# Summing two weight blocks by an adding load from GpSimd, in place of a VectorE addition, in a feed-forward with seven products

## The chip, the cores and the metric

The kernel runs on one core of one Trainium2 chip. The metric is the time of the device for one execution of the whole program, in microseconds, as the median of several runs. A core has five engines that work through their own instruction lists in order: PE (matmuls), DVE (VectorE, elementwise), ACT (ScalarE), POOL (GpSimd) and SP (SyncE, which here only issues loads and stores). Loads and stores are carried by 16 DMA engines; a load is issued from SP, or from GpSimd, and lands some microseconds later.

## What is computed

One layer of a decoder on 512 tokens of width 1024, in float32: two attention branches merged by gates, an output projection with a residual, then the part that matters here, a SwiGLU feed-forward, and a last normalization.

```python
u2 = rms_norm(x, norm_ffn_g[i])
g_ff, up_ff = jnp.split(u2 @ w_ffn_in[i], 2, axis=-1)      # 1024 x 5632
x = x + (jax.nn.silu(g_ff) * up_ff) @ w_ffn_out[i]
return rms_norm(x, norm_final_g)
```

## The kernel before

**Matmuls in three parts.** Each float32 operand is split in two: a rounded part hi (ACT, L143) and the rest lo = value - hi (DVE, L144). A product is then three matmuls: hi by hi, hi by lo, lo by hi (L767 to L769 for the feed-forward's first products, L158 to L160 for all others).

**Seven products in place of eight.** The feed-forward runs over 22 blocks of 128 hidden columns (`hidden(i)`, one call is a step below). In a step the gate's and the up part's 1024 x 128 weights, each halved along the input width, form a 2 x 2 block matrix, and the tokens in two halves the other one. The product of the two is made by a scheme with seven block products in place of eight. It needs, besides the loaded blocks, sums of weight blocks. Four weight pairs (hi, lo) are prepared for a step, in this order:

- A1: the loaded gate weights, as they are.
- S23: two blocks. The first is (up block 1 + up block 2) + gate block 1, the second is up block 1 + gate block 1.
- S1: two blocks, the sum (up block 1 + up block 2), and up block 2.
- S4: one block, the first of S23 plus gate block 2.

**Where the sum comes from.** `dma_chunk` (L104) allocates for the up weights a tile `rawu` of three thirds of 512 columns, of which there are two buffers. SP loads the two up blocks into the second and third of them with one load of 512 KB (L108). In `split_chunk` (L116) DVE adds these two into the first third (L133). Then DVE makes S23 from the first two thirds and the gate weights (L135), and later S4 (L140). S1 is read straight from the first and the last third (L137); its subtraction (L144, shown as wlo<-rawu) is the last reader of the tile, so it frees the buffer for the load of two steps later.

**What sets the order.** `weights(i, ahead=2)` (L146) is called by each product for its own weight pair; it first issues the loads up to four weight pairs ahead of the one to be split, and prepares pairs up to two ahead, at high priority. There are three buffers for hi and three for lo, so a cast waits until PE has left the product of three pairs before. On PE the order in the feed-forward is as written (L896). On the other engines, SP's and GpSimd's queues included, a planner sets the order when the kernel is built: it goes by priority and by the times at which it expects operands to be ready. On the chip each engine keeps that order, and waits for semaphores.

**What else is near.** Between the `in` steps stand `out` steps (`down`, L852), plain products with the second weight matrix, one or two after each step from step 6 on. GpSimd has little to do in the feed-forward: the power for the row factors of the normalization (`row_factors`, L276) in step 1 and at the end, and additions of squares at the end (L868). PE waits for the power's result, in its order, at L289.

Of the kernel before, what the change touches and what calls it, by code (L numbers as in the profile page):

```python
# [14 lines left out]
ALU = mybir.AluOpType  # L15

P = 128
S = 512
# [25 lines left out]
def trunk_kernel(ctx, tc, xT, gains, w_in, w_up, w_o, w_f, w_d, bias, out):  # L44
# [5 lines left out]
    nc = tc.nc  # L50
    V, A, G, T = nc.vector, nc.scalar, nc.gpsimd, nc.tensor
# [52 lines left out]
    def dma_chunk(i):  # L104
        kind, ap, n = chunks[i]
        if kind == "S23":
            r = fpool[0].tile([P, 3, S], F32, tag="rawu", name=f"rawu{i}", bufs=2)
            nc.sync.dma_start(out=r[:, 1:3, :].rearrange("p a n -> p (a n)"), in_=ap)  # L108
        elif ap is not None:
            r = wp.tile([P, 1024], F32, tag="raw", name=f"raw{i}", bufs=RAW)  # L110
            nc.sync.dma_start(out=r[:, :n], in_=ap)
        else:
            return
        raws[i] = r

    def split_chunk(i):  # L116
        kind, _, n = chunks[i]
        if i < len(chunks) - 1 and i != first_s4:
            hi = wp.tile([P, 1024], F32R, tag="whi", name=f"whi{i}")
            lo = wp.tile([P, 1024], F32R, tag="wlo", name=f"wlo{i}")  # L120
        else:
            pair_ = wide(f"w{i}", F32R)
            hi, lo = pair_[:, 0, :], pair_[:, 1, :]
        parts[i] = (hi, lo)
        hi, lo = hi[:, :n], lo[:, :n]
        if kind == "plain":
            r = raws.pop(i)[:, :n]
        elif kind == "A1":
            r = raws[i]
        elif kind == "S23":  # L130

            u = raws[i]
            V.tensor_tensor(out=u[:, 0, :], in0=u[:, 1, :], in1=u[:, 2, :], op=ALU.add)  # L133
            r = raws["S23"] = wide(f"s23{i}")
            V.tensor_tensor(out=r, in0=u[:, 0:2, :], in1=raws[i - 1][:, :S].unsqueeze(1).to_broadcast([P, 2, S]), op=ALU.add)  # L135
        elif kind == "S1":
            r = raws.pop(i - 1)[:, 0:3:2, :]  # L137
        else:
            r = fpool[0].tile([P, S], F32, tag="s4", name=f"s4{i}", bufs=1)
            V.tensor_tensor(out=r, in0=raws["S23"][:, 0, :], in1=raws.pop(i - 3)[:, S:], op=ALU.add)  # L140
        if kind in ("S23", "S1"):
            hi, lo = (t.rearrange("p (a n) -> p a n", a=2) for t in (hi, lo))
        A.copy(hi, r)  # L143
        V.tensor_tensor(out=lo, in0=r, in1=hi.bitcast(F32), op=ALU.subtract)  # L144

    def weights(i, ahead=2):  # L146
        with tc.high_priority() if i > 4 else nullcontext():
            while state["split"] <= min(i + ahead, len(chunks) - 1):
                j = state["split"]
                while state["dma"] <= min(j + (2 if chunks[j][0] == "plain" else 4), len(chunks) - 1):  # L150
                    dma_chunk(state["dma"])
                    state["dma"] += 1
                split_chunk(j)
                state["split"] += 1
        return parts[i]
# [34 lines left out]
    def wide(name, dt=F32):  # L190
        return tp.tile([P, 2, S], dt, tag="t4", name=name, bufs=N4)
# [810 lines left out]
```

## Time and profile before

| | |
|---|---|
| median of three runs | 769.46 us (769.3 to 771.01) |
| the profiled execution's own time | 769.63 us |
| its span, first to last instruction | 767.9 us |
| mean granted TensorE clock | 0.996 |
| PE, DVE, ACT, POOL busy | 751.9, 512.7, 360.3, 28.1 us |
| read from HBM | 71.32 MB |

The profile is of one execution. Its times are counted from the first instruction. A row of the timeline gives the start, the length, the engine, the line of the kernel, the operation and its tiles as out<-in; in brackets stands how long the engine had been idle, and what ended that. A row of a group gives count, busy time and mean length, then the idle time in front of it. A row of waits gives the engine and line that waited, what it waited for, microseconds in total, times, and the longest. A tile's name leaves its number out: `rawu` is any of the 22.

### The profile page before, as it was taken

How to read it: one execution, taken by the hardware profiler on the slowest of the kernel's cores; microseconds unless marked ns; L12 is line 12 of the kernel's file. 1: busy time of each engine (PE TensorE's matmuls, PEld its weight loads, DVE VectorE, ACT ScalarE, POOL GpSimd, SP SyncE). 2: the span in 40 equal slices, each digit the busy share in tenths (PEclk: the TensorE clock that was granted, in tenths of full speed). 3: DMA queues.
4: the chain of work that ended last, by engine and by line, in shares of the span. 5: the costliest groups of instructions: out<-in, count | busy, mean ns of one | idle time of the engine just before them, and what ended most of it. 6: DMA issues, size and time to landing. Idle time of an engine off the chain costs nothing. (4 is left out here: it accounts for less than half of the span.)

```text
span 767.9 us, 10991 instructions
## 1 busy us (share of the span) xinstructions
PE 751.9 (98%) x4471; PEld 644.0 (84%) x4471; DVE 512.7 (67%) x694; ACT 360.3 (47%) x515; POOL 28.1 (4%) x39
## 2 busy tenths in 40 slices
PE   8999999999999999999999999999999999999994
PEld 5876767798877878888789999999999999999983
DVE  5443746344677774368798989877788777776543
ACT  7264727563132343233454766544444554444362
POOL 1000000000100100000000000000000000000032
PEclk9999999999999999999999999999999999999998
DMA  7412121123224223233422232323333333331213
GB/s 246 137 56 82 55 83 55 55 78 114 83 84 164 83 83 102 69 103 111 164 83 83 84 103 83 117 76 121 100 103 96 104 103 113 106 107 46 65 46 111
DMA packets 24947, 74.13 MB, mean 97 GB/s; under 512 B 2736, under 2 KB 5824, under 8 KB 24768
## 3 DMA queue, kind: packets, MB, share of 16 engines
q1 hardware_dynamic: 23536, 69.74, 28.2%
q0 software_dynamic: 816, 3.16, 1.2%
q8 instruction: 35, 0.57, 0.3%
q10 hardware_dynamic: 544, 0.52, 0.2%
q14 instruction: 16, 0.13, 0.1%
HBM read 71.32 MB, written 2.10 MB: 96 GB/s over the span
## 5 line engine op out<-in xcount | busy, mean ns | idle before, releaser
L143 ACT CAST whi<-raw 128x1024 fp32r<-128x1024 f32 (+2 forms) x113 | 108.5, 962 | 157.8 <-issue 49.2
L144 DVE TENSOR_TENSOR wlo<-raw,whi 128x1024 fp32r<-128x1024 f32 (+2 forms) x113 | 125.9, 1115 | 37.7 <-ACT whi L143 37.0
L767 PE MATMUL pf<-fh,whi 128*128 128x256 f32 x348 | 99.5, 286 | 0.4 <-ACT q L774 0.4
L769 PE MATMUL pf<-fh,wlo 128*128 128x256 f32 x348 | 98.6, 283 | 0.0
L768 PE MATMUL pf<-fl,whi 128*128 128x256 f32 x348 | 98.5, 283 | 0.0
L767 PE MATMUL pg<-fh,whi 128*128 128x256 f32 x264 | 75.1, 284 | 0.6 <-ACT q L774 0.6
L768 PE MATMUL pg<-fl,whi 128*128 128x256 f32 x264 | 74.7, 283 | 0.0
L769 PE MATMUL pg<-fh,wlo 128*128 128x256 f32 x264 | 74.7, 283 | 0.0
L767 PEld LDWEIGHTS pf<-fh,whi 128*128 128x128 f32 x348 | 66.7, 192 | 2.0 <-ACT q L774 0.9
L768 PEld LDWEIGHTS pf<-fl,whi 128*128 128x128 f32 x348 | 66.7, 192 | 1.1 <-issue 0.5
L769 PEld LDWEIGHTS pf<-fh,wlo 128*128 128x128 f32 x348 | 66.7, 192 | 0.3 <-DVE wlo L144 0.2
L144 DVE TENSOR_TENSOR wlo<-s,whi 128x1024 fp32r<-128x1024 f32 (+1 forms) x43 | 41.2, 959 | 16.0 <-ACT whi L143 15.8
L767 PEld LDWEIGHTS pg<-fh,whi 128*128 128x128 f32 x264 | 50.6, 192 | 1.1 <-ACT q L774 0.8
L143 ACT CAST whi<-s 128x1024 fp32r<-128x1024 f32 (+1 forms) x43 | 36.2, 841 | 31.5 <-PE pg L768 19.6
L769 PEld LDWEIGHTS pg<-fh,wlo 128*128 128x128 f32 x264 | 50.6, 192 | 0.0
L768 PEld LDWEIGHTS pg<-fl,whi 128*128 128x128 f32 x264 | 50.6, 192 | 0.0
L158 PE MATMUL pd<-hh,whi 128*128 128x512 f32 (+1 forms) x132 | 50.4, 381 | 0.0
L159 PE MATMUL pd<-hl,whi 128*128 128x512 f32 (+1 forms) x132 | 50.3, 381 | 0.0
L160 PE MATMUL pd<-hh,wlo 128*128 128x512 f32 (+1 forms) x132 | 50.1, 379 | 0.0
L143 ACT CAST whi<-rawu 128x1024 fp32r<-128x1024 f32 x22 | 23.1, 1050 | 29.6 <-PE pd L159 25.0
L861 DVE TENSOR_TENSOR res<-pd,res 128x512 f32<-128x512 f32 (+1 forms) x36 | 22.6, 628 | 18.9 <-PE pd L160 18.8
L160 PEld LDWEIGHTS pd<-hh,wlo 128*128 128x128 f32 x132 | 24.8, 188 | 4.8
(472 smaller groups left out, 1738.8 us busy)
## 6 DMA issues: line engine op xcount, KB each, us to landing
raw<-in_w_in_dram SPq DMA_DIRECT2D x44, 512.0 KB, 3.3
rawu<-in_w_ffn_in_dram SPq DMA_DIRECT2D x22, 512.0 KB, 3.2
raw<-in_w_ffn_in_dram SPq DMA_DIRECT2D x22, 512.0 KB, 3.3
raw<-in_w_ffn_out_dram SPq DMA_DIRECT2D x24, 384.0 KB, 3.1
raw<-in_w_out_dram SPq DMA_DIRECT2D x8, 512.0 KB, 3.3
raw<-in_w_up_dram SPq DMA_DIRECT2D x8, 384.0 KB, 3.0
x<-in_xT_dram SPq DMA_DIRECT2D x8, 256.0 KB, 4.9
res<-in_xT_dram POOLq DMA_DIRECT2D x8, 256.0 KB, 4.1
```

The lines of the kernel that those rows point to most:

```text
L143: A.copy(hi, r)
L144: V.tensor_tensor(out=lo, in0=r, in1=hi.bitcast(F32), op=ALU.subtract)
L158: T.matmul(ps, shi, mhi, start=first, stop=False)
L159: T.matmul(ps, shi, mlo, start=False, stop=False)
L160: T.matmul(ps, slo, mhi, start=False, stop=last)
L767: T.matmul(ps, hi[:, cs], xhi, start=first and k == 0, stop=False, skip_group_check=True)
L768: T.matmul(ps, hi[:, cs], xlo, start=False, stop=False, skip_group_check=True)
L769: T.matmul(ps, lo[:, cs], xhi, start=False, stop=last and k == 3, skip_group_check=True)
L861: V.tensor_tensor(out=x, in0=ps, in1=x, op=ALU.add)
```

## The change

The addition at L133 goes. The first third of `rawu` is filled by two loads of 256 KB: SP loads up block 1 into it, and GpSimd loads up block 2 with addition into the same place. The old load of both blocks into the other two thirds stays. All lines behind move by two or three.

```diff
@@ dma_chunk
         if kind == "S23":
             r = fpool[0].tile([P, 3, S], F32, tag="rawu", name=f"rawu{i}", bufs=2)
+
+            nc.sync.dma_start(out=r[:, 0, :], in_=ap[:, :S])
+            nc.gpsimd.dma_start(out=r[:, 0, :], in_=ap[:, S:], accum_op=ALU.add)
             nc.sync.dma_start(out=r[:, 1:3, :].rearrange("p a n -> p (a n)"), in_=ap)
@@ split_chunk
             u = raws[i]
-            V.tensor_tensor(out=u[:, 0, :], in0=u[:, 1, :], in1=u[:, 2, :], op=ALU.add)
             r = raws["S23"] = wide(f"s23{i}")
             V.tensor_tensor(out=r, in0=u[:, 0:2, :], in1=raws[i - 1][:, :S].unsqueeze(1).to_broadcast([P, 2, S]), op=ALU.add)
```

## The prediction

> **What bounds the kernel now.** I read the page's first part, then the engines' busy time by stage, then what the tensor engine waited for, then the queues around the changed line.
>
> ```profile
> span 767.9 us, 10991 instructions
> PE 751.9 (98%) x4471; PEld 644.0 (84%) x4471; DVE 512.7 (67%) x694; ACT 360.3 (47%) x515; POOL 28.1 (4%) x39
> ```
>
> ```profile
> 366.00:414.00 48.00, 46.96 (x233) 39.30 (x232) 41.07 (x61) 26.07 (x38) 0.00 (x0) 1.00 0.31 103
> 414.00:482.00 68.00, 67.60 (x546) 65.92 (x545) 61.70 (x100) 41.70 (x69) 1.06 (x1) 1.00 0.30 98
> 482.00:723.00 241.00, 241.00 (x1656) 225.27 (x1655) 181.55 (x259) 113.20 (x172) 0.00 (x0) 1.00 0.31 96
> ```
>
> The columns after the stretch and its length are PE, PEld, DVE, ACT and POOL busy, the clock, the DMA share and GB/s. The changed line runs only in these three stretches. PE is full in the last, and has 1.44 us without a matmul in the first two together. The clock is 1.00. DVE is busy 41.07 of 48.00, then 61.70 of 68.00 (91%), then 181.55 of 241.00 (75%). So DVE is the second-fullest engine, and in the middle stretch it has little room.
>
> ```profile
> PE pg L767 <- ACT q L774: 0.6, 1, 0.6
> PE po L158 <- DVE res L728: 0.4, 1, 0.4
> PE pf L767 <- ACT q L774: 0.4, 1, 0.4
> ```
>
> These are all of PE's waits from 366 to 723 us. None of them is for a feed-forward weight that DVE prepares. Their sum, 1.4 us, is the same as the time without a matmul just read, and the most that a faster preparation could return there.
>
> **What is removed.** The addition at L133, once in each of the 22 steps:
>
> ```profile
> L133 DVE TENSOR_TENSOR rawu<-rawu 128x512 f32<-128x512 f32 x22 | 15.2, 691 | 16.2 <-DMA rawu<-in_w_ffn_in_dram 16.1
> ```
>
> That is 22 x 0.691 = 15.2 us of DVE work, and 16.1 us in which DVE stood at this line until the load had landed. Both are DVE time beside a full PE: DVE's 31.3 us lie under PE's matmuls, and PE waited for none of it. Worth of the removal on the path: 0.
>
> **What is added.** Per step SP issues a 256 KB load into the first third of the tile, GpSimd a 256 KB load that adds into the same bytes, and the old 512 KB load follows.
>
> ```profile
> rawu<-in_w_ffn_in_dram SPq DMA_DIRECT2D x22, 512.0 KB, 3.2
> res<-in_xT_dram POOLq DMA_DIRECT2D x8, 256.0 KB, 4.1
> raw<-in_w_ffn_out_dram SPq DMA_DIRECT2D x8, 256.0 KB, 2.7
> bt<-in_bias_dram POOLq DMA_DIRECT2D x1, 1024.0 KB, 5.1
> ```
>
> Traffic: 22 x 0.5 MB = 11.5 MB in the 357 us from 366 to 723, 32 GB/s on top of some 98, so the DMA share goes from 0.31 to about 0.41, an estimate in proportion. That is far from full, and costs nothing by itself. SP's extra issue stands ahead of the old load, which therefore starts one issue later (the rows below show 0.33 us); the loads queued behind it on SP move by the same.
>
> Latency: the adding load reads what the first one wrote, so GpSimd waits for the landing. The first takes 2.7 us (a 256 KB load of SP). The price of an adding load stands in no row. Its lower bound is a plain 256 KB load of GpSimd, 4.1 us. Its upper bound is two of these after one another, 8.2, if the destination must be fetched first. I take 4.4: it moves the bytes of a 512 KB load, and GpSimd's rows rise by 1.0 us from 256 to 1024 KB, a third of that for 256 KB more. The sum is then complete 2.7 + 4.4 = 7.1 us after SP's issue (6.8 to 10.9), against 3.2 us of load and 0.69 us of addition before.
>
> The serial order is where a rule of the Trainium skill speaks against the change. "DMA: Bandwidth & Descriptors", section "Rules for kernel authors", says that nothing holds the bytes between an accumulating transfer's read and its write, so that it must wait for the earlier transfer's semaphore. By it the two landings add up, as in my sum; were they ordered by the queues alone, the slower one would count. The same page's section "Anatomy of one DMA — SWDGE (gpsimd) path" prices a GpSimd transfer at 2.0 us and the bytes at 436 GB/s, 2.6 us for 256 KB, which would make the chain 5.3; the row measures 4.1 for the plain kind, so the row is what I use.
>
> **Where that latency meets DVE.** The wait moves from L133 to L135, the next reader of the sum, and DVE works in a fixed order: what stands behind L135 waits with it. Here are the steps 4 to 7, in the order load, L135, the subtraction for the step before, and the first matmul that needs its result:
>
> ```profile
> 431.45 0.33 SPq L108 DMA_DIRECT2D rawu<-in_w_ffn_in_dram  x1
> 437.52 1.22 DVE L135 TENSOR_TENSOR s<-rawu,raw 128x1024 f32<-128x1024 f32 x1
> 439.32 1.21 DVE L144 TENSOR_TENSOR wlo<-s,whi 128x1024 fp32r<-128x1024 f32 x1
> 442.42 0.28 PE L769 MATMUL pf<-fh,wlo 128*128 128x256 f32 x1
> ...
> 442.37 0.33 SPq L108 DMA_DIRECT2D rawu<-in_w_ffn_in_dram  x1
> 449.28 1.22 DVE L135 TENSOR_TENSOR s<-rawu,raw 128x1024 f32<-128x1024 f32 x1
> 450.75 1.22 DVE L144 TENSOR_TENSOR wlo<-s,whi 128x1024 fp32r<-128x1024 f32 x1
> 452.65 0.28 PE L769 MATMUL pf<-fh,wlo 128*128 128x256 f32 x1
> ...
> 453.79 0.33 SPq L108 DMA_DIRECT2D rawu<-in_w_ffn_in_dram  x1
> 459.17 1.22 DVE L135 TENSOR_TENSOR s<-rawu,raw 128x1024 f32<-128x1024 f32 x1
> 460.97 1.21 DVE L144 TENSOR_TENSOR wlo<-s,whi 128x1024 fp32r<-128x1024 f32 x1
> 463.58 0.28 PE L769 MATMUL pf<-fh,wlo 128*128 128x256 f32 x1
> ...
> 464.02 0.33 SPq L108 DMA_DIRECT2D rawu<-in_w_ffn_in_dram  x1
> 469.07 1.22 DVE L135 TENSOR_TENSOR s<-rawu,raw 128x1024 f32<-128x1024 f32 x1
> 471.20 1.21 DVE L144 TENSOR_TENSOR wlo<-s,whi 128x1024 fp32r<-128x1024 f32 x1
> 473.80 0.28 PE L769 MATMUL pf<-fh,wlo 128*128 128x256 f32 x1
> ```
>
> The tolerance of a step is the time from its load to that matmul, less the time from L135's start to the subtraction's end. Step 5: 452.65 - 442.37 = 10.28, less 451.97 - 449.28 = 2.69, leaves 7.6 us. Steps 4, 6 and 7 in the same way: 8.0, 6.8 and 6.4. If the DVE order stayed as it is, 7.1 us would be late by 0.3 and 0.7 us in steps 6 and 7 and by nothing in 4 and 5: a mean of 0.25, over seven early steps (2 to 8, the four shown taken for all) 1.8 us.
>
> But L135's own result isn't urgent there. The sum of step 5, made at 449.28, is for a product a full step later, since the subtraction at 450.75 still serves step 4. The order on DVE isn't written out by hand (only PE's is); it is planned from expected times when the kernel is built. L133's place shows that such plans reckon with a load's flight:
>
> ```profile
> DVE rawu L133 <- DMA rawu<-in_w_ffn_in_dram: 16.1, 17, 3.9
> ```
>
> In 17 of 22 steps it waited for the landing, 0.9 us on average, so it stands about where the data is expected. With two flights in a row I expect L135 to be placed some 3 us later, behind the subtractions for the step before, where its wait blocks nothing urgent. The cover is then the rest of a step, about 3 us more. Value taken: 0. If that cover is missing, it costs the 1.8 us above at my latency, and the prices of the first rival at more.
>
> Later steps have more room. From step 9 on L135 stands further from its load; the shortest such distance that I found is step 14's:
>
> ```profile
> 566.96 0.33 SPq L108 DMA_DIRECT2D rawu<-in_w_ffn_in_dram  x1
> 577.02 1.22 DVE L135 TENSOR_TENSOR s<-rawu,raw 128x1024 f32<-128x1024 f32 x1
> ```
>
> 10.06 us, which holds 7.1 and all but the top of its range.
>
> **GpSimd's queue.** It gets 22 waits for a landing. Behind them could stand the row factors' power at L276:
>
> ```profile
> 417.66 0.33 SPq L108 DMA_DIRECT2D rawu<-in_w_ffn_in_dram  x1
> ...
> 423.77 1.06 POOL L276 TENSOR_TENSOR r<-ms,mh 128x4 f32<-128x4 f32 x1 [146.03 <-DVE ms L268]
> ...
> 426.14 1.02 PE L289 MATMUL rb<-dg,ones 128*128 128x512 f32 x2
> ```
>
> PE waits for it, and PE works in order. The load of step 4 can't be issued before PE has gone past that matmul: its buffer comes free with the third weight pair of step 2, whose own buffer PE empties in the last products of step 1, behind the matmul. So the adding load of step 4 can't stand ahead of the power without a deadlock. That of step 3 can be issued at 417.66 + 2.7 = 420.4, 3.4 us before the power. Cost 0, unless GpSimd needs more than those 3.4 us to issue a transfer.
>
> **The sum.** The profiled execution took 769.63 us, of which 767.9 are the span; the median of three is 769.46. 769.63 - 0 + 0 = 769.6 us. A measurement of this kernel tells about 0.3% (2.3 us) from no change.
>
> **Rivals.** First, slower: L135 keeps a place ahead of an urgent subtraction, and the latency exceeds 7.2 us, the mean tolerance of the four steps. Then DVE stands with urgent work behind it and PE stops. At an adding load of 5.5 us the chain is 8.2, the four steps are late by 0.2, 0.6, 1.4 and 1.8 us, mean 1.0; over seven steps 7 us: 777. At the upper bound of 8.2 the chain is 10.9, 3.7 us a step and 26 us, with step 14 and its like touched as well: 796 or more. For it: DVE is 91% busy in this stretch, so little drains a backlog, and in the profile DVE already waited 16.1 us at L133, so the plan's times are somewhat short of the chip's. Against: the urgency lies elsewhere, and the planner can move L135. Chance 0.30, and 0.08 more for an adding load dearer than its upper bound or a late sum in all 22 steps, at 790 and beyond.
>
> Second, faster: DVE, freed of 15.2 us, delivers everything else earlier, and PE's three waits go. That returns at most their 1.4 us: 768.2, still within the bound of no change. A gain over 2.3 us would need PE itself to issue its matmuls faster, for which I see nothing; I leave 0.05 for a new order of the planned engines that helps in the last 45 us, at 767.
>
> Third, the change only moves the wait: DVE's 16.1 us of standing reappear at L135 in the same size or larger, and DVE's idle time isn't smaller. This is compatible with my forecast; it gives 769.6 as well.
>
> **How the numbers follow.** No change 0.57 (769.6, with a gain of 1.4 us or the 1.8 us of the unmoved order still inside 2.3 us), slower 0.30 + 0.08 = 0.38, faster 0.05. The range from 768.0 to 779.0 holds the first case, and the first rival to about 8.5 us of chain, some 0.22 of its 0.30, together 0.79; left out are the dearest cases and a real gain. The likeliest case's own range is 768.0 to 771.8.
>
> **What would show it.** Right: DVE has 22 fewer additions, its busy time is some 15 us lower, PE's rows in 482 to 723 still read 241.00, no wait of PE on wlo appears, and the adding loads land about 4.4 us after issue. Right in part: DVE waits at L135 for the adding load, with no late matmul. Wrong: PEld or PE waits for wlo or for the cast between 410 and 485, a landing above 6 us, or a matmul at L289 that starts late after the power on GpSimd. A time below 767 would mean that DVE had delayed PE in a way that the waits don't show.

## The result, and the profile after

The changed kernel takes 790.89 us (median of 4 runs, 789.99 to 792.56), the kernel before 769.39 us (4 runs). The ratio is 1.0273, with a 95% interval of 1.0260 to 1.0286: slower by 21.5 us, and outside the range of the prediction. The profiled execution took 791.53 us.

The first part of the page after, and the engines' busy time in stretches that answer to the three of before. Columns are as there: PE, PEld, DVE, ACT, POOL, clock, DMA share, GB/s.

```profile
span 789.8 us, 11096 instructions
PE 761.2 (96%) x4471; PEld 649.3 (82%) x4471; DVE 499.6 (63%) x672; ACT 360.1 (46%) x515; POOL 47.3 (6%) x61
```

```profile
366.00:414.00 48.00, 47.83 (x235) 40.06 (x234) 38.28 (x58) 25.14 (x37) 2.26 (x3) 1.00 0.45 137
414.00:504.00 90.00, 75.37 (x553) 71.03 (x552) 60.05 (x95) 43.54 (x72) 6.80 (x8) 0.94 0.40 112
504.00:745.00 241.00, 241.00 (x1656) 225.25 (x1656) 174.08 (x246) 113.21 (x173) 11.23 (x13) 1.00 0.44 124
```

The last stretch is the same as before to the last figure: 241.00 us, 1656 matmuls, PE full, although DMA's share rose from 0.31 to 0.44. So neither the traffic nor the later steps lost time. The middle one grew from 68 to 90 us for some 550 matmuls. In it PE stands 14.63 us, and the granted clock is 0.94. The loads date the loss: at step 1's load on SP the changed kernel's profile is 1.75 us late (367.62 against 365.87), which comes from its start and not from the change (last section); at step 4's it is 11.79 us late (443.24 against 431.45), at step 8's 21.98 (496.23 against 474.25), and 21.9 at the end. So the loss of the change lies between the products of step 1 and those of step 7, one half ahead of step 4's load and one half behind it.

What PE waited for in the changed kernel, with DVE's wait for the new loads (in total, times, longest):

```profile
DVE s L137 <- DMA rawu<-in_w_ffn_in_dram: 23.5, 7, 5.1
...
PE rb L291 <- ACT dg L286: 8.4, 3, 5.6
POOL r L278 <- issue: 7.9, 1, 7.9
...
PE pf L769 <- ACT q L776: 5.5, 3, 2.5
...
PE pf L771 <- DVE wlo L146: 2.1, 3, 1.1
```

L137 is the old L135, the reader of the sum; L291 and L278 are the old L289 and L276. Two places are new. DVE stands 23.5 us at the reader, in 7 of the steps, and PE then waits on what DVE does behind it: 2.1 us on `wlo`, 5.5 us on a PSUM bank (where PE's products collect) that ACT empties into the kept tile `q`, which it can overwrite only when DVE's `g` has read it. And PE waits 5.6 us at once for the row factors, whose power on GpSimd stood 7.9 us without anything that the profile shows to wait for. The loads themselves, by the page (KB each, median us from issue to landing):

```profile
rawu<-in_w_ffn_in_dram SPq DMA_DIRECT2D x22, 512.0 KB, 4.1
...
rawu<-in_w_ffn_in_dram SPq DMA_DIRECT2D x22, 256.0 KB, 3.2
rawu<-in_w_ffn_in_dram POOLq DMA_DIRECT2D x22, 256.0 KB, 3.9
```

**Step 5 in the changed kernel**, from its first load to the late matmuls:

```profile
456.09 0.33 SPq L109 DMA_DIRECT2D rawu<-in_w_ffn_in_dram  x1
...
459.81 0.42 DVE L829 SCALAR_TENSOR_TENSOR u<-q,yv 128x256 f32<-128x256 f32 x1
459.91 0.86 POOL L110 DMA_DIRECT2D rawu<-in_w_ffn_in_dram  x1 [11.80 <-DVE wlo L146]
...
465.37 1.23 DVE L137 TENSOR_TENSOR s<-rawu,raw 128x1024 f32<-128x1024 f32 x1 [5.14 <-DMA rawu<-in_w_ffn_in_dram]
466.51 0.42 DVE L828 TENSOR_TENSOR g<-pg,q 128x256 f32<-128x256 f32 x1
467.02 0.37 ACT L776 COPY q<-pf 128x256 f32<-128x256 f32 x1 [3.97 <-DVE g L828]
...
467.18 1.22 DVE L146 TENSOR_TENSOR wlo<-s,whi 128x1024 fp32r<-128x1024 f32 x1
...
467.44 0.39 PE L769 MATMUL pf<-fh,whi 128*128 128x256 f32 x1 [2.48 <-ACT q L776]
468.45 0.38 PE L771 MATMUL pf<-fh,wlo 128*128 128x256 f32 x1 [0.50 <-DVE wlo L146]
...
468.98 1.22 DVE L146 TENSOR_TENSOR wlo<-rawu,whi 128x1024 fp32r<-128x1024 f32 x1
```

The sum is there 465.37 - 456.09 = 9.3 us after SP's issue. DVE has the reader directly behind `u`, one place earlier than before, where `g` came first. Everything below it in DVE's order waits with it, ACT's copy waits for `g`, and PE stands 2.48 + 0.50 us. The granted clock is then at 0.50 for some 3.4 us. The last row is the subtraction that frees the other of the two buffers. The load of step 6 goes out behind it, at 470.22.

**The row factors**, at the end of step 1's products:

```profile
425.79 0.84 POOL L110 DMA_DIRECT2D rawu<-in_w_ffn_in_dram  x1 [11.38 <-DVE s L142]
...
430.66 0.16 DVE L270 TENSOR_SCALAR ms<-ss 128x4 f32<-128x4 f32 x1
...
434.58 1.05 POOL L278 TENSOR_TENSOR r<-ms,mh 128x4 f32<-128x4 f32 x1 [7.95 <-issue]
...
436.41 2.08 PE L291 MATMUL rb<-dg,ones 128*128 128x512 f32 x2 [5.56 <-ACT dg L286]
```

The power's input is there at 430.82, and the power begins at 434.58, 7.95 us after GpSimd issued its adding load. In the instruction list that the build makes for GpSimd, an instruction of the kind that loads code stands directly ahead of this power. The profile doesn't list it. Before, it stood directly behind the last load of `res` (the residual), at 278 us, in the 146 us that GpSimd idled; in the changed kernel four adding loads stand between that load of `res` and it. What PE does after this wait:

```profile
436.00:438.00 2.00, 1.59 (x3) 0.84 (x3) 1.61 (x7) 1.88 (x5) 0.00 (x0) 0.50 0.00 0
438.00:440.00 2.00, 2.00 (x10) 1.72 (x9) 1.48 (x2) 0.00 (x0) 0.00 (x0) 0.50 0.00 0
440.00:442.00 2.00, 2.00 (x11) 2.00 (x11) 1.63 (x5) 1.07 (x2) 0.00 (x0) 0.50 0.00 0
...
444.00:446.00 2.00, 2.00 (x19) 2.00 (x18) 1.91 (x4) 1.73 (x5) 0.00 (x0) 1.00 0.79 265
```

PE reads as busy, but at a clock of 0.50 it does 10 or 11 matmuls in 2 us instead of 19.

### The profile page after: what moved, and what is told of

The parts are those of the page before. It is cut to its first block, busy times and chain, and to the rows that moved or that the text cites. A ratio compares the mean times of both kernels' runs of the same rounds, so it can differ in the third digit from the quotient of the medians.

```text
span 789.8 us, 11096 instructions
## 1 busy us (share of the span) xinstructions
PE 761.2 (96%) x4471; PEld 649.3 (82%) x4471; DVE 499.6 (63%) x672; ACT 360.1 (46%) x515; POOL 47.3 (6%) x61
## 4 chain that ended last, share of the span: by engine, by line
PE 87%; DMA 5%; DVE 4%; ACT 1%; issue 1%; SPq 0%; POOL 0%; DVEq 0%; POOLq 0%; ACTq 0%
PE pd L160 5%; PE pd L161 5%; PE pd L162 5%; PE pf L771 4%; PE pf L769 4%; PE pf L770 4%; DMA rawu<-in_w_ffn_in_dram 4%; PE pg L769 3%; PE pg L770 3%; PE pg L771 3%; PE pjgs L160 2%; DVE wlo L146 2%; PE pjgd L160 2%; PE pjgs L162 2%; PE pjgd L162 2%; PE po L160 2%
## 5 line engine op out<-in xcount | busy, mean ns | idle before, releaser
L769 PE MATMUL pf<-fh,whi 128*128 128x256 f32 x348 | 101.1, 291 | 6.4 <-ACT q L776 5.5
L137 DVE TENSOR_TENSOR s<-rawu,raw 128x1024 f32<-128x1024 f32 x22 | 26.9, 1222 | 26.0 <-DMA rawu<-in_w_ffn_in_dram 23.5
L110 POOL DMA_DIRECT2D rawu<-in_w_ffn_in_dram x22 | 19.2, 885 | 396.3 <-DMA rawu<-in_w_ffn_in_dram 308.1
```

Source lines behind the costliest of these rows:

```text
L110: nc.gpsimd.dma_start(out=r[:, 0, :], in_=ap[:, S:], accum_op=ALU.add)
L769: T.matmul(ps, hi[:, cs], xhi, start=first and k == 0, stop=False, skip_group_check=True)
```

## The experiments

My theory was that two stalls make the loss: DVE standing at the reader of the sum, and GpSimd's code load that came to lie behind an adding load. Rivals were the traffic itself, the price of an adding load, and, later, each step's lateness taken by itself. The letters in each expectation are those that it defines. Ratios are against the kernel before, run on the same chip, with their 95% intervals. Gains of one changed kernel over another are differences of bare medians; where the two ran in different batches, whose kernels before took 769.4 to 770.6 us, the difference of their excesses is up to 0.7 us larger.

### The power's code loaded early

The changed kernel, with one more small power on GpSimd, of constants, that nothing reads. It stands behind the last load of `res`, so that the code is there before the adding loads.

```diff
+    early = cp.tile([P, 8], F32)
+    pw = G.tensor_tensor(out=early, in0=mh, in1=mh, op=ALU.pow)
+    tc.add_manual_dep(pw.ins, last.ins.name, NOSYNC, reason="issue order")
```

> The change, and a power of eight constants on GpSimd behind the last load of the residual, near 278 us. It makes the code load that stands ahead of the row factors' power happen there, where GpSimd idles. Theory A (two causes: DVE stands at the sum's reader in steps 2 to 8, and GpSimd's code load has moved behind the adding load of step 3, so that PE waits for the row factors and then runs at half clock for a while): the power starts within 0.3 us of its input, PE's wait of 5.6 us at the row factors' matmul shrinks below 2, and 791 falls by 4 to 7 us, to 784 to 787. Rival B (only DVE's standing counts, the power's lateness comes from DVE): no change, 790 to 791. Rival C (the traffic of the extra loads slows the weights down): no change, 790 to 791.

788.2 us, ratio 1.0244 (1.0223 to 1.0264). The timeline of this kernel:

```profile
286.88 1.68 POOL L661 TENSOR_TENSOR early<-mh 128x8 f32<-128x8 f32 x1 [8.27 <-issue]
...
429.35 1.23 DVE L137 TENSOR_TENSOR s<-rawu,raw 128x1024 f32<-128x1024 f32 x1 [4.76 <-DMA rawu<-in_w_ffn_in_dram]
430.49 0.16 DVE L270 TENSOR_SCALAR ms<-ss 128x4 f32<-128x4 f32 x1
...
430.73 1.95 POOL L278 TENSOR_TENSOR r<-ms,mh 128x4 f32<-128x4 f32 x1 [4.90 <-DVE ms L270]
```

The 8.27 us moved to the early power, and the real one now starts 0.08 us after its input. So the pause was the code load, and not work of the adding load. But the input `ms` stands behind the reader on DVE, which waited 4.76 us. So PE still waits 3.3 us there, after which the clock is at half for 6.8 us, and the kernel gains only 2.7 us, where I expected 784 to 787.

### The reader placed later

The changed kernel, with one ordering edge and no semaphore: the reader of the sum stands on DVE behind the subtraction that frees the other buffer (S1 of the step before).

```diff
+            s23 = V.tensor_tensor(...)          # the reader
+            if "after" in state:
+                tc.add_manual_dep(s23.ins, state["after"].ins.name, NOSYNC, reason="issue order")
...
+        sub = V.tensor_tensor(out=lo, in0=r, in1=hi.bitcast(F32), op=ALU.subtract)
+        if kind == "S1":
+            state["after"] = sub
```

> The change, with the sum's reader on DVE held behind the subtraction of the third weight pair of the step before, by an edge for the planner alone. Theory A: DVE's waits for the adding load go to under 2 us, the late steps' PE waits go, but GpSimd's code load still stands behind the adding load of step 3: 776 to 780. Rival B: 769 to 771, since DVE no longer stands. Rival C: 788 to 791.

777.91 us, ratio 1.0111 (1.0096 to 1.0126): 13.0 us of the 21.5 come back. DVE has no wait for `rawu` left. What stays is GpSimd's pause, and PE's wait and half clock behind it:

```profile
431.38 1.05 POOL L282 TENSOR_TENSOR r<-ms,mh 128x4 f32<-128x4 f32 x1 [7.99 <-issue]
...
433.21 2.07 PE L295 MATMUL rb<-dg,ones 128*128 128x512 f32 x2 [4.86 <-ACT dg L290]
```

### Both edits

> The change with both edits, the early power and the late reader. Theory A: 769 to 771, the same as before, with all 22 adding loads in place. Rival B: also 769 to 771. Rival C: 788 to 791, because every byte of the traffic is still there.

771.03 us (10 runs), ratio 1.0014 (1.0004 to 1.0024). The power now starts on its input, behind the same adding load:

```profile
420.59 0.86 POOL L110 DMA_DIRECT2D rawu<-in_w_ffn_in_dram  x1 [8.86 <-DVE u L837]
423.58 1.04 POOL L282 TENSOR_TENSOR r<-ms,mh 128x4 f32<-128x4 f32 x1 [2.14 <-DVE ms L274]
```

All 44 new loads are still there, with all their traffic, and 20 of the 21.5 us are gone. So neither the traffic nor the price of an adding load makes the loss; together they are worth some 1 us (0.3 to 1.8 by the interval). DVE's busy time in this kernel is 500.5 us against 512.7 before, and that brings nothing. The two edits alone give 2.7 and 13.0 us, and together 19.9: the stalls overlap at the row factors, where the reader of step 3's sum holds up the power's input and the code load the power, and each hides part of the other.

### The adding loads only from step 8 on

Steps 0 to 7 keep the old addition.

> The adding loads in steps 8 to 21 only; steps 0 to 7 keep the addition on DVE. Theory A: 769 to 771, since neither the early steps' tight order nor the power's place on GpSimd is touched, with DVE some 9 us less busy; nothing gained, because PE is full there. Rival C: two thirds of the loss stay, 780 to 784.

769.50 us (10 runs), ratio 0.9990 (0.9979 to 1.0002). With the change in fourteen of the 22 steps nothing is lost, and nothing gained.

### One pair of new loads that nobody reads

The kernel before, with the two new loads once, in step 3, into spare bytes. DVE's addition stays. The computation is as before, the two loads are extra work.

```diff
+            if k == 3:
+                x = fpool[0].tile([P, S], F32, tag="form", name=f"spare{i}", bufs=2)
+                new = nc.sync.dma_start(out=x, in_=ap[:, :S])
+                tc.add_manual_dep(new.ins, old.ins.name, NOSYNC, reason="issue order")
+                nc.gpsimd.dma_start(out=x, in_=ap[:, S:], accum_op=ALU.add)
```

> The kernel before, its additions on DVE in place, with one added pair: in step 3 alone SP loads a block into spare bytes that nothing reads, and GpSimd adds another into it. Theory A: the code load for the power stands behind this adding load, the power starts some 8 us after the adding load was issued, about 431, PE waits 4 to 5 us at the row factors' matmul and then runs at half clock for about 6 us: 776 to 779. Rival B (only DVE's standing counts): 769 to 771, since nobody reads the sum.

780.52 us, ratio 1.0127 (1.0112 to 1.0142): a single adding load costs 9.9 us.

```profile
424.28 0.92 POOL L114 DMA_DIRECT2D spare<-in_w_ffn_in_dram  x1 [145.21 <-PE pg L775]
433.87 1.05 POOL L282 TENSOR_TENSOR r<-ms,mh 128x4 f32<-128x4 f32 x1 [8.66 <-issue]
...
435.70 2.07 PE L295 MATMUL rb<-dg,ones 128*128 128x512 f32 x2 [8.17 <-ACT dg L290]
```

It does so only by its place: it stands ahead of the code load, which can now begin at 425.20, and the power starts 8.66 us later. PE waits 8.17 us of them, since here DVE isn't late and nothing else hides the pause. My 776 to 779 were short by 1.5 us at the top: I had taken PE's wait to be 4 to 5 us, near the 5.56 of the changed kernel.

### One flight in place of two

SP's first load left out, and GpSimd's load plain: the first third then holds up block 2 alone and not the sum, so up block 1 is missing where S23, S1 and S4 use the sum of both. DVE's reader stands ahead of the subtractions for the step before, as in the change, and GpSimd's loads have the same places in its queue.

```diff
-            nc.sync.dma_start(out=r[:, 0, :], in_=ap[:, :S])
-            nc.gpsimd.dma_start(out=r[:, 0, :], in_=ap[:, S:], accum_op=ALU.add)
+            nc.gpsimd.dma_start(out=r[:, 0, :], in_=ap[:, S:])
```

> The change without SP's first load, and GpSimd's load plain: one flight in place of two in series, by the same queue, with DVE's addition gone as in the change. The first third then holds the second block alone and not the sum. Theory A (two flights in series are what DVE stands for): DVE's waits at the reader fall from 23.5 us to under 6, the power is late by about 3 us only, since GpSimd needn't wait for a landing; 771 to 776. Rival D (a load on GpSimd's queue is slow or late as such): 784 to 791.

773.01 us, ratio 1.0037 (1.0023 to 1.0050). With one flight DVE waits 2.2 us at the reader in the whole feed-forward. The code load is still late (a pause of 8.12 us), but the load ahead of it is issued at 419.37, without a first flight to wait for, so the power comes at 428.03 and PE waits 2.11 us. So it is the two flights in series that make the change expensive, and not the reader's move to a GpSimd load. The addition went with the first flight here, but it prices little by itself: the median landing is 3.7 us for these plain loads and 3.9 for the adding ones.

### The later reader, with PE kept busy

The kernel with the later reader, and 22 matmuls of zeros on PE ahead of the row factors' matmul, whose result nobody reads.

```diff
+        for _ in range(22):
+            T.matmul(pw, warm, warm.unsqueeze(1).to_broadcast([P, 4, P]), start=True, stop=True)
```

> The late reader of the second experiment, and 22 matmuls of zeros on PE just ahead of the row factors' matmul, some 5 us that fill PE's wait there. They change no result that is read. Theory A with its half clock: PE never stands for long, its clock stays at 1.00, and the about 3 us lost at half clock come back: 777.9 falls to 774 to 776. If the half clock costs nothing, or has another cause: 777 to 779.

775.52 us, ratio 1.0065 (1.0049 to 1.0082), 2.4 us less than without them. The same stretches, first of the kernel with the later reader alone, then of this one:

```profile
432.00:434.00 2.00, 0.79 (x1) 0.50 (x2) 1.50 (x7) 1.54 (x6) 0.43 (x1) 0.50 0.00 0
434.00:436.00 2.00, 2.00 (x7) 1.26 (x6) 1.22 (x4) 0.94 (x2) 0.00 (x0) 0.50 0.00 0
```

```profile
432.00:434.00 2.00, 2.00 (x8) 0.86 (x7) 1.75 (x8) 1.78 (x6) 0.18 (x1) 1.00 0.00 0
434.00:436.00 2.00, 2.00 (x19) 2.00 (x18) 1.55 (x3) 1.22 (x2) 0.00 (x0) 1.00 0.00 0
```

The clock stays at 1.00. So of the 6.9 us that lie between this later reader (777.9) and both edits (771.0), some 2.4 are the half clock that follows PE's wait, and the rest the wait itself, which the added matmuls fill for 4.9 us.

### Steps 4 to 7: each by itself, or handed on

Two kernels with the adding loads from step 8 on, and besides in steps 4 and 6, or in 4 to 7. No adding load stands ahead of the power, so the code load stays where it was before.

```diff
-            if k >= 8:
+            if k in (4, 6) or k >= 8:       # the second kernel: if k >= 4
```

> The adding loads only in steps 4 and 6 and from 8 on; steps 0 to 3, 5 and 7 keep the old addition, so that no adding load stands ahead of the row factors' power. Theory A, a loop through the two buffers: while DVE waits for the sum of one step, the subtraction that frees the other buffer stands behind it, so the next load starts late by as much, and the lateness is handed on from step to step. With an old step in between, whose load takes 3 to 4 us, it is made good: 770 to 772 us. Theory B, every step by itself, the time from load to matmul less DVE's own work as the prediction has it (8.0 and 6.8 us in these steps against sums after 8.0 and 7.5 us): 0.7 us, 770 to 771. Theory C, each adding load among steps 2 to 7 costs the same 2 to 3 us: 774 to 776.

> The adding loads in all steps from 4 on, the old addition in steps 0 to 3. Theory A, the loop: a step lasts as long as the sum's two flights and DVE's 4.9 us from the reader of the sum to the end of the subtraction that frees the next load's buffer, 12.7 to 14.1 us with flights of 7.5 to 9.3, where a step of PE lasts 10.9: 7 to 9 us over four steps, 776.5 to 779.5. Theory B, every step by itself: 0 + 1.7 + 0.7 + 2.1 = 4.5 us by the flights of the changed kernel, 773.5 to 775.5. Theory C, each adding load costs the same: twice what the other kernel of this call loses, 778 to 782.

774.83 us, ratio 1.0057 (1.0041 to 1.0073), for steps 4 and 6; 780.25 us, ratio 1.0129 (1.0111 to 1.0148), for 4 to 7. By the totals alone theory C fits best, 4.9 and 10.3 us: both lie in its ranges, and in neither case in A's or B's. The trace speaks against an equal price for each load. The time from one step's load on SP to the next step's load, from the timeline's rows:

| us | 4 to 5 | 5 to 6 | 6 to 7 | 7 to 8 | sum |
|---|---|---|---|---|---|
| before | 10.92 | 11.42 | 10.23 | 10.23 | 42.80 |
| changed | 12.85 | 14.13 | 12.66 | 13.35 | 52.99 |
| later reader | 11.25 | 9.89 | 10.93 | 10.22 | 42.29 |
| steps 4 and 6 | 12.51 | 10.22 | 14.28 | 10.04 | 47.05 |
| steps 4 to 7 | 12.65 | 13.03 | 14.44 | 12.39 | 52.51 |

In the kernel with steps 4 and 6, step 4 makes the next load 1.6 us later than before (12.51 against 10.92). PE doesn't stand for it, and step 5, an old one, regains 1.2 us of it. Step 6 then loses 4.05 us, because its sum came late, after 464.94 - 455.51 = 9.4 us:

```profile
455.51 0.33 SPq L111 DMA_DIRECT2D rawu<-in_w_ffn_in_dram  x1
...
464.94 1.23 DVE L142 TENSOR_TENSOR s<-rawu,raw 128x1024 f32<-128x1024 f32 x1 [4.99 <-DMA rawu<-in_w_ffn_in_dram]
...
467.01 0.38 PE L774 MATMUL pf<-fh,whi 128*128 128x256 f32 x1 [2.17 <-ACT q L781]
468.01 0.39 PE L776 MATMUL pf<-fh,wlo 128*128 128x256 f32 x1 [0.51 <-DVE wlo L151]
```

PE stands 2.17 + 0.51 = 2.7 us, and the clock is 0.64 in the four us from 468 and 0.93 in the next four, 3.4 us at half, worth 1.7. Together that is 4.4. So neither A's nor B's number for this kernel was right: both had taken 7.5 us for step 6's sum.

Steps 4 to 7 tell A from B. The kernel's first two steps:

```profile
431.82 0.33 SPq L111 DMA_DIRECT2D rawu<-in_w_ffn_in_dram  x1
...
439.62 1.23 DVE L142 TENSOR_TENSOR s<-rawu,raw 128x1024 f32<-128x1024 f32 x1 [1.77 <-DMA rawu<-in_w_ffn_in_dram]
...
443.22 1.22 DVE L151 TENSOR_TENSOR wlo<-rawu,whi 128x1024 fp32r<-128x1024 f32 x1
444.47 0.33 SPq L111 DMA_DIRECT2D rawu<-in_w_ffn_in_dram  x1
...
452.65 1.23 DVE L142 TENSOR_TENSOR s<-rawu,raw 128x1024 f32<-128x1024 f32 x1 [4.20 <-DMA rawu<-in_w_ffn_in_dram]
...
454.72 0.39 PE L774 MATMUL pf<-fh,whi 128*128 128x256 f32 x1 [1.74 <-ACT q L781]
455.73 0.39 PE L776 MATMUL pf<-fh,wlo 128*128 128x256 f32 x1 [0.50 <-DVE wlo L151]
```

Step 5's sum is there after 8.18 us, 0.6 beyond the prediction's tolerance of 7.6, yet PE stands 2.24 us. The missing 1.6 to 1.7 us are those by which step 5's load was late (12.65 against 10.92): DVE's wait in step 4, for which PE did not stand, had been handed on. The way is to be seen in the rows: from the reader's start to the next load are 444.47 - 439.62 = 4.85 us, DVE's work down to the subtraction that frees the other buffer. So in these rows a step lasts at least flight + 4.85. In this kernel 7.80 + 4.85 = 12.65 and 8.18 + 4.85 = 13.03, and in the changed kernel 9.28 + 4.85 = 14.13 for step 5. Before, a step lasts 42.80 / 4 = 10.7 us, which leaves 10.7 - 4.85 = 5.85 us for the sum, and the sums take 7.5 to 9.4. Over four steps that makes 9.7 us (52.51 - 42.80), and the kernel loses 10.3. B's 4.5 us falls. A has the way right and the size too low: 0.75 us above its top here, and 2.8 above it with steps 4 and 6, where it had the sum too early. C's equal price doesn't hold: the lateness by steps is 1.6 us, mostly regained, and 4.05 in the one kernel, and 1.7, 1.6, 4.2 and 2.2 us in the other.

## Why the prediction was wrong

**What held.** PE bounds the kernel, and DVE's removed work is worth nothing: its busy time fell by 13.1 us (15.2 were removed), and no kernel here gained from it. The steps from 8 on lose nothing. The first flight takes 3.2 us (2.7 said), the adding load 3.9 (4.4 said), DMA's share is 0.44 (0.41 said). The wait moved from the addition to the reader, L135 before and L137 now, as the third rival has it: 16.1 us of standing became 23.5.

**First failed step: "Value taken: 0" for the wait at L135.** Three things in it were wrong. The planner did not put the reader behind the subtractions for the step before. It left it where it was or within one place of it, in steps 5 and 6 one place earlier. What I took for its reckoning with the flight, the waits at L133, says nothing of these steps: in steps 4 to 6 L133 waited for no landing, and stood 3.8 to 5.0 us behind its load (435.40 - 431.45, 447.41 - 442.37, 457.63 - 453.79). Where an edge puts the reader behind them by hand, DVE doesn't wait at all, and 13.0 us return: my reason was right about the place, but nothing showed that the planner would choose it. Next, the tolerance of 7.2 us counted each step from a load that was on time, whereas the next load waits for a subtraction that stands behind the reader. Over the loop through two buffers the room is 5.85 us, so that even my own sum of 7.1 us would have lost 1.25 us a step where I reckoned 0.25. The rows for it stood in the prediction itself: the next load follows the reader's start there by 442.37 - 437.52 = 4.85 us. Last, the sum took 7.0 to 9.3 us in steps 2 to 7 of the changed kernel and not 7.1, although the two medians give 7.1 (3.2 + 3.9): GpSimd's row mostly begins some 0.6 us behind the first landing (in step 5, 459.91 - 456.09 = 3.82 us after SP's row), and some of these adding loads land later than the median (in step 5, 465.37 - 459.91 = 5.5 us from GpSimd's row to the reader).

**Second failed step: "Cost 0" for GpSimd's queue.** I reckoned that the adding load could be issued before the power, and took the power's pause of 146.03 us for idling only. It also hid a code load. Moved behind the adding load, that takes 8 us; alone it costs some 7 to 10 (6.9 from later reader to both edits, 9.9 for the single unread load), of which 2.4 are PE's half clock. My condition was an issue that takes over 3.4 us. The issue itself takes 0.84; what stands behind it does not fit. Both signs that the prediction gave for this and for the first step came: PE waits for `wlo`, and the row factors' matmul starts late behind the power. The third, a landing above 6 us, did not (5.8 at most).

**The rivals.** The first rival, a reader that keeps its place ahead of urgent work, is what happened, and it had a chance of 0.30. Its price was too low: at a sum after 8.2 us it gave 1.0 us a step, and the loop gives 8.2 - 5.85 = 2.35. The 0.08 for 790 and beyond named other causes than the one that led there.

**What stays open.** PE waited on two results behind the reader, the bank through `g` and `q`, and `wlo`, and no run parted them. Nor is it shown why some adding loads land late. In the changed kernel those of steps 5, 7 and 8, beside which SP issues another weight load within 0.3 us, landed 5.4, 4.7 and 4.7 us after their row began, those of steps 2, 3, 4 and 6 after 3.6 to 4.2; no run moved the neighbours. A third buffer for `rawu`, which would cut the loop in another way, wasn't tried: with this kernel's other tiles it doesn't fit into SBUF. The 1.0 us that both edits leave is not explained. And no version here is faster than the kernel before.

## What to carry to other kernels

Where an in-order engine waits for a load, look for what frees the next load's buffer: if that stands behind the wait, the flight and the work behind it add up to a loop, and its length has to be set against a step of the bounding engine, not the slack of one step against one flight. Two loads that must follow each other make such a loop longer by a whole flight, and an edge that moves the waiting reader behind the freeing operation can be worth more than the change itself. A long idle time on an engine may hide preparation that isn't listed; before anything is queued ahead of it, look into that engine's instruction list.

## What the runs showed of the hardware

- **GpSimd's code load.** Ahead of a power that follows other GpSimd code, 7.95 to 8.66 us pass after the instruction before it in the queue (7.95, 7.99, 8.06, 8.12, 8.27, 8.31, 8.66 in seven kernels), and no row shows them. A second power behind it has no such pause. The Trainium skill's "GPSIMD Engine Reference", section "2.1 Instruction dispatch", says that the first call to freshly loaded code pays about 6 us that no profile instruction shows. These runs agree on what is hidden and measure a third to nearly a half more.
- **The clock after a wait.** Where PE waited 3.31, 4.86, 5.56 and 8.17 us the granted clock fell to 0.50 for some 6.8 us, beginning within the wait. After shorter waits it was halved for some 3.4 us, or not at all: halved after 2.48 + 0.50 us (step 5 of the changed kernel), 2.17 + 0.51 (step 6 of the kernel with steps 4 and 6) and 1.18 + 0.50 (step 6 of the kernel with the early power), and at 1.00 after 2.11 (one flight) and 1.74 + 0.50 us (steps 4 to 7). So the length of a wait alone didn't decide it. The Trainium skill's "TensorE: Matmul & The Clock Gate", section "What's actually happening", has the clock at half after an idle window of about 3.4 us, and at full again after as long a busy one. The half clock's lengths, one or two times 3.4 us, agree; waits shorter than 3.4 us were enough in several cases.
- **An adding load lands hardly later than a plain one**: 3.9 us median from the start of its issue in the changed kernel and 3.7 with both edits, against 3.7 for GpSimd's plain load of the same bytes in the kernel with one flight, though GpSimd's issue row, which is part of it, is longer: 0.84 to 1.13 us against mostly 0.54.
- **The start.** In most profiles, but not in those of the kernel before, of both edits and of steps 4 to 7, the clock is 0.91 from 20 to 40 us, long before a changed line runs. In the changed kernel's profile that answers to the 1.75 us by which it is late at step 1's load, and it is no part of the change: the kernel with both edits has all the loads and not this.
